# Moving a mode switch four tiles later, and splitting the last three tiles' heads differently, in a bias + logsumexp kernel

## Chip, cores, metric

One NeuronCore of a Trainium2 chip. The metric is device time in microseconds (us) of one execution. Ratios are the mean time of one kernel's fast runs over the mean of the other's fast runs of the same rounds, so they are not quite the ratio of the medians quoted beside them.

## The reference

```python
# x: (8, 2048, 2048) fp32 = batch, row, 8 heads of 256;  bias: (8, 256)
x_heads = x.reshape(B, S, H, Dh).transpose(0, 2, 1, 3) + bias[None, :, None, :]
x_tiled = np.repeat(x_heads, 2, axis=2)          # each row's result is written twice
mx = x_tiled.max(axis=-1, keepdims=True)
out = mx.squeeze(-1) + np.log(np.exp(x_tiled - mx).sum(axis=-1))
```

The kernel leaves the maximum out (the inputs are normal draws) and computes log(sum(exp(x + bias))), over 64 tiles of 128 x 2 rows of 2048 numbers, 2.1 MB each.

## The kernel before: the parts concerned

There are three ways to bring the bias in. *Heads below `pe`*: TensorE adds it in its accumulator memory (PSUM), ScalarE exponentiates and sums, one activation per head and row. *Heads from `g0`*: GpSimd adds it in place, ScalarE exponentiates, VectorE reduces. *Heads between*: ScalarE exponentiates x alone and VectorE multiplies by exp(bias): in bulk (`late=True`) by one multiplication and one reduce a tile later, otherwise at once by one weighted sum per head and row (`weigh`), whose result a short second instruction reads out. With `g0=8` no head goes to GpSimd.

```python
BULK = dict(pe=2, g0=4, late=True)
MIXED = dict(pe=1, g0=5, late=False)
PROMPT = dict(pe=2, g0=8, late=False)
#         from tile, mode, halves: each of the two rows loaded and worked on by itself
STAGES = [(0, BULK, False), (49, MIXED, False), (57, MIXED, True), (61, PROMPT, True)]
LAST_CUTS = [[0, 512, 1280, 2048], [0, 512, 1536, 2048]]   # pieces of tile 63's two rows
...
    def later(m, xt, k0, k1, sums):                    # one piece later
        h0 = m["pe"] if m["late"] else m["g0"]
        v = xt[:, k0:k1, h0 * Dh : D]
        exp_inplace(v)
        if m["late"]:
            ...   # VectorE: heads h0 to g0 times exp(bias), in place
        nc.vector.tensor_reduce(out=sums[:, k0:k1, h0:H], ...)
...
    for t in range(T):
        ...
        for k0, k1, c0, c1 in pieces(t):
            if c0 == 0:
                got = add_bias(m, xt, k0, k1)          # TensorE
                if m["g0"] < H:
                    g_add(m, xt, k0, k1)               # GpSimd
            if for_pool:
                for_pool()                             # `later` of the piece before
            ...
                exp_inplace(xt[:, k0:k1, h0 * Dh : h1 * Dh])
            if for_pe and (c0 == 0 or c1 == D):
                for_pe()                               # ScalarE's own heads, a row late
            ...
                        weigh(...)                     # VectorE, per head and row
            # (cut) for_pool and for_pe are set; load(t + 9) follows the release of the buffer
```

The softmax here doesn't subtract the row's maximum and nothing guards it: scores larger than these inputs give would overflow.

## Time and profile before

| | before |
|---|---|
| time, median of 3 runs | 332.10 us (332.07 to 332.19) |
| profiled span | 330.5 us |
| DMA queue | full until about 319 us, loads of x landed by 323 us |
| VectorE's last read-out | 326.01 us |
| store issued; end of the span | 327.13; 330.5 us |

The groups by form give the price of VectorE's work. Columns: line, engine, operation, names, partitions x elements, count, then busy us and mean ns of one, then idle time before it.

```profile
L228 DVE TENSOR_REDUCE R<-xt 128x12 f32<-128x3072 f32 x49 | 164.4, 3355 | 5.8 <-DVE xt L222 1.0
L222 DVE TENSOR_TENSOR xt<-xt,w_ps 128x1024 f32<-128x1024 f32 x49 | 59.6, 1217 | 29.9 <-ACT xt L212 29.8
L240 DVE CUSTOM_DVE_ANT_0 junk<-xt,w_ps 128x256 f32<-128x256 f32 x114 | 40.6, 417 | 1.2 <-ACT xt L212 1.1
```

A bulk tile is one of each of the first two lines, 4.57 us. A weighted sum (third line) lasts 417 ns, but in a run the next starts 343 ns after it; sums of work here use the distance between starts. The order of VectorE's work and the end of the kernel are shown in the prediction.

### The profile page before, as it was taken

How to read it: one execution, taken by the hardware profiler on the slowest of the kernel's cores; microseconds unless marked ns; L12 is line 12 of the kernel's file. 1: busy time of each engine (PE TensorE's matmuls, PEld its weight loads, DVE VectorE, ACT ScalarE, POOL GpSimd, SP SyncE). 2: the span in 40 equal slices, each digit the busy share in tenths (PEclk: the TensorE clock that was granted, in tenths of full speed). 3: DMA queues.
4: the chain of work that ended last, by engine and by line, in shares of the span. 5: the costliest groups of instructions: out<-in, count | busy, mean ns of one | idle time of the engine just before them, and what ended most of it. 6: DMA issues, size and time to landing. Idle time of an engine off the chain costs nothing.

```text
span 330.5 us, 2287 instructions
## 1 busy us (share of the span) xinstructions
PE 228.9 (69%) x383; PEld 65.3 (20%) x383; DVE 288.3 (87%) x380; ACT 291.4 (88%) x567; POOL 270.7 (82%) x79
## 2 busy tenths in 40 slices
PE   6498675695759667689667796866686645665780
PEld 2132121121212221222211221221121110132220
DVE  0019999999999999999999999998889999999994
ACT  3279999899999999989999889998999998999894
POOL 6999999979989999899999999988998667786300
PEclk9997977579775977955898558777857555555585
DMA  7999999999999999999999999999999999999970
GB/s 293 433 426 434 426 429 426 430 424 428 420 435 425 430 428 426 431 427 430 425 428 426 428 428 428 428 428 427 428 428 429 426 432 415 421 420 421 418 277 17
DMA packets 11744, 135.42 MB, mean 410 GB/s; under 512 B 1425, under 2 KB 1553, under 8 KB 2769
## 3 DMA queue, kind: packets, MB, share of 16 engines
q1 hardware_dynamic: 11632, 135.27, 96.9%
q14 instruction: 11, 0.09, 0.1%
q8 instruction: 3, 0.05, 0.1%
q10 hardware_dynamic: 2, 0.01, 0.0%
q0 software_dynamic: 96, 0.00, 0.0%
HBM read 134.23 MB, written 1.05 MB: 409 GB/s over the span
## 4 chain that ended last, share of the span: by engine, by line
DMA 61%; ACT 14%; issue 7%; POOL 6%; PE 6%; DVE 5%; DVEq 0%; POOLq 0%; SPq 0%; ACTq 0%
DMA xt<-in_x_dram 58%; ACT xt L212 10%; PE ps L177 4%; POOL xt L207 4%; ACT ps L189 4%; DVE xt L222 3%; DVE R L228 2%; DMA b<-bparts 2%; PE ps L167 1%; DMA brow<-in_bias_dram 1%; DVE junk L240 1%; POOL brest L132 0%; POOL brest L130 0%; POOL b L135 0%; PE tpair L258 0%
## 5 line engine op out<-in xcount | busy, mean ns | idle before, releaser
L207 POOL TENSOR_TENSOR xt<-xt,b_rep 128x2048 f32<-128x2048 f32 (+2 forms) x65 | 264.3, 4068 | 35.9 <-DMA xt<-in_x_dram 26.9
L177 PE MATMUL ps<-xt,ident 128*128 128x512 f32 (+1 forms) x240 | 174.6, 859 | 72.1 <-DMA xt<-in_x_dram 71.7
L212 ACT ACTIVATE xt<-xt 128x3072 f32<-128x3072 f32 (+3 forms) x89 | 184.6, 2095 | 10.0 <-POOL xt L207 8.1
L228 DVE TENSOR_REDUCE R<-xt 128x12 f32<-128x3072 f32 (+1 forms) x56 | 176.6, 3154 | 5.8 <-DVE xt L222 1.0
L189 ACT ACTIVATE ps<-ps 128x256 f32<-128x256 f32 x232 | 85.7, 369 | 15.5 <-PE ps L177 10.8
L222 DVE TENSOR_TENSOR xt<-xt,w_ps 128x1024 f32<-128x1024 f32 x49 | 59.6, 1217 | 29.9 <-ACT xt L212 29.8
L177 PEld LDWEIGHTS ps<-xt,ident 128*128 128x128 f32 x240 | 53.5, 252 | 153.9 <-DMA xt<-in_x_dram 113.6
L167 PE MATMUL ps<-b,ones 3*128 3x512 bf16 (+1 forms) x120 | 48.7, 471 | 9.9 <-ACT ps L189 6.0
L189 ACT ACTIVATION_READ_ACCUMULATOR ps<-ps 128x1 f32 x232 | 44.1, 190 | 0.0
L240 DVE CUSTOM_DVE_ANT_0 junk<-xt,w_ps 128x256 f32<-128x256 f32 x114 | 40.6, 417 | 1.2 <-ACT xt L212 1.1
L167 PEld LDWEIGHTS <-ones 3*128 3x128 bf16 x120 | 7.8, 98 | 79.7 <-issue 79.7
L228 DVE TENSOR_REDUCE R_last<-xt 128x3 f32<-128x768 f32 (+1 forms) x9 | 9.4, 1042 | 0.0
L258 PE MATMUL tpair<-ident,R 128*64 128x128 f32 x14 | 3.7, 360 | 7.7 <-DVE R L228 6.2
L240 DVE CUSTOM_DVE_ANT_0 junk<-xt,w_sb 128x256 f32<-128x256 f32 x18 | 6.7, 422 | 0.0
L240 DVE DVE_READ_ACCUMULATOR2_ANT R_last<- 128x1 f32 x76 | 6.5, 85 | 0.0
L139 PE MATMUL ps<-brow,ones 1*128 1x512 f32 x4 | 3.7, 1088 | 3.2 <-DMA brow<-in_bias_dram 3.2
L145 ACT ACTIVATE b_rep<-ps 128x512 f32<-128x512 f32 x2 | 1.2, 598 | 4.4 <-PE ps L139 4.4
L240 DVE DVE_READ_ACCUMULATOR2_ANT R<- 128x1 f32 x56 | 4.7, 84 | 0.0
L268 ACT ACTIVATE res<-tpair 64x512 f32<-64x512 f32 x7 | 4.1, 581 | 0.4 <-PE tpair L258 0.4
L139 PE MATMUL w_ps<-brow,ones 1*128 1x512 f32 x4 | 4.0, 1096 | 0.7 <-ACT w_ps L151 0.7
L258 PEld LDWEIGHTS tpair<-ident,R 128*64 128x64 f32 x14 | 1.4, 134 | 14.9 <-DVE R L228 11.9
L151 ACT ACTIVATE w_ps<-w_ps 128x512 f32<-128x512 f32 x2 | 1.2, 582 | 3.3 <-PE w_ps L139 3.3
(21 smaller groups left out, 12.4 us busy)
## 6 DMA issues: line engine op xcount, KB each, us to landing
xt<-in_x_dram SPq DMA_DIRECT2D x57, 2048.0 KB, 31.8
xt<-in_x_dram SPq DMA_DIRECT2D x12, 1024.0 KB, 20.8
out_dram<-res SPq DMA_DIRECT2D x7, 128.0 KB, 31.3
xt<-in_x_dram SPq DMA_DIRECT2D x3, 256.0 KB, 15.7
xt<-in_x_dram SPq DMA_DIRECT2D x2, 384.0 KB, 15.9
xt<-in_x_dram SPq DMA_DIRECT2D x1, 512.0 KB, 12.2
out_dram<-res_last SPq DMA_DIRECT2D x1, 128.0 KB, 1.7
b<-bparts POOLq DMA_DIRECT2D x3, 1.0 KB, 5.8
```

The source lines that it names most:

```text
L139: nc.tensor.matmul(dst, lhsT=ones, rhs=brow[:, c0:c1], start=True, stop=True)
L145: nc.scalar.activation(out=b_rep[:, c - G0 : c - G0 + MM], in_=ps[i], func=ACT.Copy)
L167: nc.tensor.matmul(p[:, 0 : (kb - ka) * n], lhsT=ones3, rhs=each_row(b3, 0, n, kb - ka), start=True, stop=False,)
L177: nc.tensor.matmul(bass.AP(tensor=p.tensor, offset=p.offset, ap=[p.ap[0], [1, (kb - ka) * n]]), lhsT=ident, rhs=xt[:, ka:kb, 0:n], start=F ...
L189: nc.scalar.activation(out=p[:, c : c + Dh], in_=p[:, c : c + Dh], func=ACT.Exp, accum_out=dst(h),)
L207: nc.gpsimd.tensor_tensor(out=v, in0=v, in1=each_row(b_rep, c - G0, D - c, k1 - k0), op=ALU.add)
L212: nc.scalar.activation(out=v, in_=v, func=ACT.Exp)
L222: nc.vector.tensor_tensor(out=f, in0=f, in1=each_row(w_ps, h0 * Dh - W0, n, k1 - k0), op=ALU.mult,)
L228: nc.vector.tensor_reduce(out=sums[:, k0:k1, h0:H], in_=v.rearrange("p k (h j) -> p k h j", j=Dh), op=ALU.add, axis=mybir.AxisListType.X,)
L240: nc.vector.tensor_tensor_reduce(out=j, in0=v, in1=w, scale=1.0, scalar=0.0, op0=ALU.mult, op1=ALU.add, accum_out=dst,)
L258: nc.tensor.transpose(out=tp[0:nr, k], in_=R[b][:, k].rearrange("p h n -> p (h n)"), identity=ident,)
L268: nc.scalar.activation(out=rs[0:nr], in_=tv, func=ACT.Ln)
```

## The change

Its intent, as I read it: the tail showed VectorE waiting for ScalarE, so ScalarE is given one head less in every other row of the last three tiles; the last row's first piece shrinks to what TensorE needs of it, and the other cuts of the last tile move with the heads; and bulk mode, with fewer VectorE instructions, is kept four tiles longer.

```diff
-PROMPT = dict(pe=2, g0=8, late=False)
-STAGES = [(0, BULK, False), (49, MIXED, False), (57, MIXED, True), (61, PROMPT, True)]
-LAST_CUTS = [[0, 512, 1280, 2048], [0, 512, 1536, 2048]]
+PROMPT2 = dict(pe=2, g0=8, late=False)
+PROMPT1 = dict(pe=1, g0=8, late=False)
+STAGES = [
+    (0, False, (BULK,)),
+    (53, False, (MIXED,)),
+    (57, True, (MIXED, MIXED)),
+    (61, True, (PROMPT2, PROMPT1)),      # row 0, row 1
+]
+LAST_CUTS = [[0, 512, 1024, 2048], [0, 256, 1280, 2048]]
```

The rest of the diff (cut) only makes the mode depend on the row as well.

## The prediction

> **What bounds the kernel now.** I first looked at the page's busy shares and slices. The load queue is full for 38 of the 40 slices, VectorE for nearly as many.
>
> ```profile
> PE 228.9 (69%) x383; PEld 65.3 (20%) x383; DVE 288.3 (87%) x380; ACT 291.4 (88%) x567; POOL 270.7 (82%) x79
> DVE  0019999999999999999999999998889999999994
> DMA  7999999999999999999999999999999999999970
> ```
>
> The reader is to see that the transfer of x (134.23 MB) fills the DMA engines until about 320 us of a span of 330.5 us. Nothing in the change alters the bytes, so until there the time is the transfer's. What can move is the stretch from the last landings to the end. Second, I listed all instructions from 311 us on, to see what ends last:
>
> ```profile
> 322.87 1.57 ACT L212 ACTIVATE xt<-xt 128x1024 f32<-128x1024 f32 x2
> 326.01 0.08 DVE L240 DVE_READ_ACCUMULATOR2_ANT R_last<- 128x1 f32 x1
> 326.24 0.45 PE L276 MATMUL tpair<-ident,R_last 128*128 128x128 f32 x1 [4.25 <-DVE R_last L240]
> 326.72 0.38 ACT L282 ACTIVATE res_last<-tpair 128x256 f32<-128x256 f32 x1 [1.40 <-PE tpair L276]
> 327.13 0.35 SPq L283 DMA_DIRECT2D out_dram<-res_last  x1
> ```
>
> The last row's exponentials on ScalarE, then VectorE's weighted sums up to 326.01, then a transpose, a logarithm and the store: 4.5 us from VectorE's last read-out to the end of the span. VectorE's end sets the kernel's end. Third, VectorE's waits, in 250 to 312 us (first line) and in 300 to 331 us (second):
>
> ```profile
> DVE xt L222 <- ACT xt L212: 0.2, 1, 0.2
> DVE junk L240 <- ACT xt L212: 1.1, 3, 0.4
> ```
>
> From 254.55 us on VectorE waits for nothing until the last rows: it works off a backlog for 64 us, and the 1.1 us of waiting comes only at the very end. So I read its order of work through that stretch; first instruction of a tile or row in each line:
>
> ```profile
> 249.72 1.21 DVE L222 TENSOR_TENSOR xt<-xt,w_ps 128x1024 f32<-128x1024 f32 x1
> 254.55 1.22 DVE L222 TENSOR_TENSOR xt<-xt,w_ps 128x1024 f32<-128x1024 f32 x1 [0.16 <-ACT xt L212]
> 255.87 3.35 DVE L228 TENSOR_REDUCE R<-xt 128x12 f32<-128x3072 f32 x1
> 259.14 0.41 DVE L240 CUSTOM_DVE_ANT_0 junk<-xt,w_ps 128x256 f32<-128x256 f32 x1
> ...
> 276.71 0.41 DVE L240 CUSTOM_DVE_ANT_0 junk<-xt,w_ps 128x256 f32<-128x256 f32 x1
> ...
> 294.27 0.41 DVE L240 CUSTOM_DVE_ANT_0 junk<-xt,w_ps 128x256 f32<-128x256 f32 x1
> ...
> 312.07 0.42 DVE L240 CUSTOM_DVE_ANT_0 junk<-xt,w_ps 128x256 f32<-128x256 f32 x1
> ```
>
> Tile 48, the last bulk one, starts at 254.55; tile 49, the first mixed one, at 259.14; tile 53 at 276.71; the half-tile rows of tile 57 at 294.27; the prompt rows of tile 61 at 312.07. Bulk tiles come at the transfer's pace: multiplications at 239.87, 244.77, 249.72 and 254.55 are 14.68 / 3 = 4.89 us apart, with 4.57 us of work in each and a short wait for ScalarE. Mixed tiles, backlogged, take (294.27 - 259.14) / 8 = 4.39 us. So in mixed mode VectorE gains 0.5 us a tile on the transfer, which in bulk mode it does not. The backlog exists because a bulk tile's sum is done one tile late and a mixed tile's first heads at once: at the switch both fall due together. Tile 49's exponential ended near 256.2, VectorE got to it at 259.14, 2.9 us behind; by tile 61 it was 0.6 us behind.
>
> **What the Trainium skill says.** "VectorE: DVE Perf Modes", section "Mode 1× (REGULAR) — the baseline", makes fp32 or PSUM operands a case of one result per cycle, at 0.96 GHz by its Specifications. 1024, 3072 and 256 elements are then 1.07, 3.20 and 0.27 us; the trace has 1.22, 3.35 and 0.42 us (0.343 us from start to start in a run), so it agrees with some 0.15 us fixed for each, and no faster form is waiting in this change. "ScalarE: Activation LUTs", "What ACT_TABLE_LOAD costs", gives 186 ns + 0.833 ns an element, with about 93 ns overlap: 1.47 us for 1536 elements, the trace 1.479 us. I use it for the one size before has not: 1792 elements, 1.68 us (estimate), 1.59 us from start to start. "GPSIMD Engine Reference", "1. Specifications", says that its SBUF interface is shared with VectorE, with contention for instructions with two SBUF inputs. Only heads 5 to 7 weighted on VectorE read both inputs from SBUF, and GpSimd's last addition ended at 309.3 us, so the trace has no case, and none should arise.
>
> **The change, part by part.**
>
> *Bulk mode to tile 53.* Four tiles swap eight weighted sums and a reduce of 1536 (4.39 us on VectorE when backlogged) for a multiplication and a reduce of 3072 at the transfer's pace of 4.89 us. GpSimd adds 2048 instead of 1536 columns, 4.54 instead of 3.45 us, still under 4.89. ScalarE does two more heads per tile's rows from PSUM; bulk tiles keep pace already. On the path is only VectorE: it reaches tile 53 at 259.14 + 4 x 4.89 = 278.70, not 276.71: +1.99 us. From there on it has fewer mixed tiles in which to catch up, and I expect it never to wait again.
>
> *Alternating two and one ScalarE heads in tiles 61 to 63.* In each odd row one head goes from ScalarE (activation and read-out, some 0.5 us) to VectorE (0.343 us) and into the big exponential (256 x 0.833 ns = 0.21 us). ScalarE is relieved of 0.3 us in each of three rows; VectorE gets 3 x 0.343 = +1.03 us. TensorE has less to do.
>
> *Cuts.* Row 0 of the last tile: exponentials of 512 and 1024 instead of 768 and 768. Row 1: first piece 256, then 1024 and 768 instead of 1024 and 512. The bytes are equal. The narrow piece needs no exponential, only TensorE. If ScalarE were the bound, its last rows would run: row 1 of tile 62 from 317.34 to 318.93, sums of two rows to 320.3, last tile's 512 and 1024 to 321.8, its sums to 322.7, then 1024 and 768 to 324.5. Before, the last exponential ended at 324.43, too. So ScalarE ends as it did.
>
> *The sum for VectorE*, from 278.70: four mixed tiles 4 x 4.39 = 17.57; eight half-tile rows of tiles 57 to 60 at (312.07 - 294.27) / 8 = 2.225, 17.80; then six and seven heads in turn for three tiles, 39 x 0.343 = 13.39 (tile 61's first six took 2.06 us). 278.70 + 17.57 + 17.80 + 13.39 = 327.46, where the last read-out begins; before 326.01. Is it ever idle? It reaches tile 61 at 314.07 (its exponential is done near 311.5), row 1 at 316.13 (ready 314.0), tile 62 at 318.53 (ready 316.4) and 320.59 (318.9), the last tile at 322.99 (320.9), its last row at 325.05 (1024 columns ready at 323.7) and that row's last three heads at 326.4 (ready 324.5). Never. Told as differences: +1.99 for the late start, +1.03 for three more heads, and -1.58 for the idle time that before had after 312.07 (13.94 us for 36 heads of 0.343 = 12.36) and that the backlog now fills: +1.44 us. The close of transpose, logarithm and store is unchanged. 332.1 + 1.44 = 333.5 us.
>
> **Rivals.**
>
> *ScalarE is the bound and is relieved.* This must be the intent: at the end VectorE did wait 1.1 us for it. If the backlog did not reach the last tile, ScalarE would reach the last row's pieces at 322.7 instead of 322.87, but seven heads instead of six follow: VectorE's end +0.15 us, and the time 332.2. With luck in how the last pieces land, 331.7. Against it: the unbroken VectorE of 64 us, which gets two microseconds more to carry.
>
> *Buffers come free later and the load queue starves.* Releases for the last loads move by up to 2 us (tile 52's buffer at 278.8 instead of 276.7). A starving queue would add up to 2 us and give 335 to 336. Against it: landings are 4.89 us apart, a full load lands 31.8 us after issue in the table of issues, so over six tiles are outstanding; and in before the half loads are held by earlier loads' landings, not by buffers. I count nothing.
>
> *The last narrow pieces land later.* Rows of 1 KB may move less well than 2 KB. Before, the last pieces landed near 322.5. A delay by 0.5 us would hide behind VectorE, which is a microsecond and more behind the data. Worth 0 to 0.3 us.
>
> *VectorE's bulk start drifts.* If the transfer's phase or a hiccup puts tile 53 at 278.2 or 279.2, the end moves one for one, as there is no idle time left to take it up: 333.0 to 334.0.
>
> **Range and chances.** The sum rests on durations that repeat to 0.01 us and on one choice, that backlog holds to the end. I leave 0.5 us each way for the start and up to 0.3 for landing, and some room for ScalarE's rival below: 332.4 to 334.4. Two per cent is 6.6 us, and no rival reaches it. Same is 0.975.
>
> **What would show it.** Right: VectorE without a wait from about 274 us to its end; tile 53's first weighted sum at 278.7; tile 61's at 314.1, two microseconds later than before; 39 weighted sums from there to the end; VectorE's waits for ScalarE in the tail gone, and the chain that ended last made of VectorE and no longer of ScalarE; ScalarE's last exponential still near 324.5; DMA landings as before. Wrong: waits of VectorE for ScalarE after 314 us (then the first rival), or a queue with gaps in the last eight slices (the second), or tile 53 at 277 or earlier, which would mean that bulk tiles can be worked faster than the transfer brings them.

## The result, and the profile after

333.46 us (333.30 to 333.56, 4 runs) against 332.13 us (4 runs) in the same rounds: ratio 1.0040, 95% interval 1.0022 to 1.0057. It is slower by 1.3 us, far within 2%.

The page of the changed kernel, its shares and two slice rows:

```profile
PE 231.2 (70%) x395; PEld 68.0 (21%) x395; DVE 289.3 (87%) x326; ACT 291.5 (88%) x573; POOL 275.0 (83%) x79
DVE  0019999999999999999999899998899899999995
DMA  8999999999999999999999999999999999999950
```

The busy shares are nearly unchanged and tell nothing: VectorE's busy time differs by 1.0 us in total. The load queue has no gap. Next VectorE's waits, in 262 to 332 us (columns: who waited for whom, us in total, times, longest), and its order, first instruction of tile 52, of tile 53, of tile 57, of tile 61, and the last:

```profile
DVE xt L228 <- ACT xt L218: 0.9, 3, 0.4
```

```profile
274.27 1.22 DVE L228 TENSOR_TENSOR xt<-xt,w_ps 128x1024 f32<-128x1024 f32 x1 [0.22 <-ACT xt L218]
...
278.87 0.41 DVE L246 CUSTOM_DVE_ANT_0 junk<-xt,w_ps 128x256 f32<-128x256 f32 x1
...
296.44 0.41 DVE L246 CUSTOM_DVE_ANT_0 junk<-xt,w_ps 128x256 f32<-128x256 f32 x1
...
314.24 0.41 DVE L246 CUSTOM_DVE_ANT_0 junk<-xt,w_ps 128x256 f32<-128x256 f32 x1
...
327.64 0.08 DVE L246 DVE_READ_ACCUMULATOR2_ANT R_last<- 128x1 f32 x1
```

All three waits are bulk multiplications, the last at 274.27. From there VectorE works for 53 us without a wait, to the end; before's three waits in the tail are gone. Tile 53 begins at 278.87 instead of 276.71. The close:

```profile
322.45 1.78 ACT L218 ACTIVATE xt<-xt 128x1024 f32<-128x1024 f32 x2
...
327.86 0.45 PE L282 MATMUL tpair<-ident,R_last 128*128 128x128 f32 x1 [5.39 <-DVE R_last L246]
328.34 0.38 ACT L288 ACTIVATE res_last<-tpair 128x256 f32<-128x256 f32 x1 [3.72 <-PE tpair L282]
328.75 0.35 SPq L289 DMA_DIRECT2D out_dram<-res_last  x1
```

ScalarE is done with the last row's exponentials at 324.23 (322.45 + 1.78) and, after its last sum, waits 3.72 us for the end, 1.40 us in before. VectorE is 1.63 us later than before's, the span only 1.15 us longer: the step from the store's issue to the end was 2.88 us, in before 3.35 us. The prediction had taken that as unchanged.

### The profile page after: what moved, and what is told of

It is laid out like the page before. It is cut to its first block, busy times and chain, and to the rows that moved or that the text cites. A ratio compares the mean times of both kernels' runs of the same rounds, so it can differ in the third digit from the quotient of the medians.

```text
span 331.6 us, 2275 instructions
## 1 busy us (share of the span) xinstructions
PE 231.2 (70%) x395; PEld 68.0 (21%) x395; DVE 289.3 (87%) x326; ACT 291.5 (88%) x573; POOL 275.0 (83%) x79
## 5 line engine op out<-in xcount | busy, mean ns | idle before, releaser
L213 POOL TENSOR_TENSOR xt<-xt,b_rep 128x2048 f32<-128x2048 f32 (+2 forms) x65 | 268.6, 4134 | 31.2 <-DMA xt<-in_x_dram 29.1
L183 PE MATMUL ps<-xt,ident 128*128 128x512 f32 (+1 forms) x248 | 177.3, 849 | 69.0 <-DMA xt<-in_x_dram 68.4
L218 ACT ACTIVATE xt<-xt 128x3072 f32<-128x3072 f32 (+4 forms) x85 | 183.2, 2172 | 11.2 <-POOL xt L213 9.2
L234 DVE TENSOR_REDUCE R<-xt 128x12 f32<-128x3072 f32 (+1 forms) x56 | 183.0, 3268 | 6.2 <-DVE xt L228 1.0
L195 ACT ACTIVATE ps<-ps 128x256 f32<-128x256 f32 x237 | 87.5, 369 | 13.5 <-PE ps L183 9.2
L228 DVE TENSOR_TENSOR xt<-xt,w_ps 128x1024 f32<-128x1024 f32 x53 | 64.4, 1216 | 31.3 <-ACT xt L218 31.3
L183 PEld LDWEIGHTS ps<-xt,ident 128*128 128x128 f32 x248 | 56.0, 255 | 151.9 <-DMA xt<-in_x_dram 104.0
L195 ACT ACTIVATION_READ_ACCUMULATOR ps<-ps 128x1 f32 x237 | 45.0, 190 | 0.0
L246 DVE CUSTOM_DVE_ANT_0 junk<-xt,w_ps 128x256 f32<-128x256 f32 x85 | 30.2, 412 | 0.0
```

What stands on the lines that cost most here:

```text
L183: nc.tensor.matmul(bass.AP(tensor=p.tensor, offset=p.offset, ap=[p.ap[0], [1, (kb - ka) * n]]), lhsT=ident, rhs=xt[:, ka:kb, 0:n], start=F ...
L195: nc.scalar.activation(out=p[:, c : c + Dh], in_=p[:, c : c + Dh], func=ACT.Exp, accum_out=dst(h),)
L213: nc.gpsimd.tensor_tensor(out=v, in0=v, in1=each_row(b_rep, c - G0, D - c, k1 - k0), op=ALU.add)
L218: nc.scalar.activation(out=v, in_=v, func=ACT.Exp)
L228: nc.vector.tensor_tensor(out=f, in0=f, in1=each_row(w_ps, h0 * Dh - W0, n, k1 - k0), op=ALU.mult,)
L234: nc.vector.tensor_reduce(out=sums[:, k0:k1, h0:H], in_=v.rearrange("p k (h j) -> p k h j", j=Dh), op=ALU.add, axis=mybir.AxisListType.X,)
```

## The experiments

The theory: VectorE runs a backlog from the switch out of bulk mode to the end, so its end is its start at the switch plus the sum of its work, less what idle time is left. (A backlog is work whose inputs are ready before the engine comes to it.) The main rival: ScalarE's last exponentials set the end. All twelve kernels gave correct results. Here "last read-out" is the start of VectorE's last instruction and "store to end" the time from the store's issue to the last instruction of the trace, both from each profile, in us. (The expectations, and the figures 2.8 and 3.4 us in them, took the second from spans rounded to 0.1 us.) The time before in the same rounds was 332.23 to 332.26 us.

| run | time, us | ratio (95%) | last read-out | store to end |
|---|---|---|---|---|
| before | 332.13 | | 326.01 | 3.35 |
| changed | 333.46 | 1.0040 (1.0022-1.0057) | 327.64 | 2.88 |
| bulk to 53 alone | 332.42 | 1.0005 (0.9993-1.0018) | 326.64 | 2.88 |
| tail alone | 332.26 | 1.0000 (0.9987-1.0012) | 325.83 | 3.33 |
| changed, old cuts | 333.59 | 1.0039 (1.0026-1.0051) | 327.80 | 2.88 |
| changed, bulk to 51 | 332.88 | 1.0021 (1.0007-1.0034) | 326.73 | 3.25 |
| changed, ScalarE loaded | 333.56 | 1.0040 (1.0027-1.0052) | 327.76 | 2.88 |
| before, ScalarE loaded | 333.78 | 1.0045 (1.0031-1.0059) | 327.54 | 3.34 |
| changed, bulk to 45 | 332.51 | 1.0008 (0.9996-1.0021) | 326.65 | 2.88 |
| two heads in tile 63 | 332.02 | 0.9990 (0.9977-1.0002) | 325.84 | 3.33 |
| changed, VectorE filled | 333.60 | 1.0042 (1.0028-1.0056) | 327.98 | 2.88 |
| before, VectorE filled | 332.87 | 1.0019 (1.0006-1.0031) | 326.50 | 3.35 |
| before, TensorE filled | 332.26 | 0.9998 (0.9982-1.0014) | 326.08 | 3.35 |
| changed, TensorE filled | 333.45 | 1.0037 (1.0022-1.0052) | 327.50 | 2.88 |

### Each half of the change alone

```diff
# bulk to 53 alone, on the kernel before
-STAGES = [(0, BULK, False), (49, MIXED, False), ...
+STAGES = [(0, BULK, False), (53, MIXED, False), ...
```

> Bulk mode to tile 53 alone, with before's prompt rows and cuts. Backlog theory (VectorE's unbroken work sets the end): VectorE reaches tile 53 at 278.8 us instead of 276.7 (+2.0), but 1.6 us of its idle time in the tail takes that up: 278.8 + 17.57 + 17.80 + 36 x 0.343 = 326.5, +0.45 us on before, so 332.6 us, and no wait of VectorE after 275 us. Rival (ScalarE's last exponentials set the end): 332.1 us. Rival (late start costs in full, one for one): 334.1 us.

```diff
# tail alone, on the changed kernel
-    (53, False, (MIXED,)),
+    (49, False, (MIXED,)),
```

> Alternating heads and new cuts, bulk mode only to tile 49 as in before. Backlog theory: VectorE reaches tile 61 at 312.1 as before, its three extra heads (1.03 us) fill idle time, and it then waits for ScalarE's 1024 columns of the last row near 323.5; seven heads from there give 326.0, so 332.1 us, within 0.3 of before. Rival (three extra heads add in full): 333.1 us. Rival (ScalarE's relief pays): 331.7 us or less.

Bulk to 53 alone: 332.42 us. The last lines of its VectorE and its queue:

```profile
326.64 0.08 DVE L240 DVE_READ_ACCUMULATOR2_ANT R_last<- 128x1 f32 x1
327.76 0.35 SPq L283 DMA_DIRECT2D out_dram<-res_last  x1
```

VectorE ends 0.63 us later than in before, near the 0.45 expected, and does not wait after 280 us. Of its 2.2 us later start (278.90) the idle time took up 1.6. Of the 0.63 us only 0.2 shows in the time, as this run, too, has the shorter close. That a late start costs in full is excluded: 0.63 us is not 2.2 us.

Tail alone: 332.26 us, as before. Its only wait in the tail, and its last read-out:

```profile
318.84 0.42 DVE L246 CUSTOM_DVE_ANT_0 junk<-xt,w_ps 128x256 f32<-128x256 f32 x1 [0.37 <-ACT xt L218]
...
325.83 0.08 DVE L246 DVE_READ_ACCUMULATOR2_ANT R_last<- 128x1 f32 x1
```

Three more heads on VectorE were free here, as expected. But the place of the wait was not the expected one: not the last row's 1024 columns near 323.5, but the second row of tile 62, at 318.84. From there 20 heads follow without a gap, 318.84 + 20 x 0.343 = 325.7. So neither half costs anything clear of noise, 0.2 and 0.0 us, and together they cost 1.3. Before has 1.6 us of idle time in the tail. The three heads alone live on it; the late start alone uses it up, and the 0.63 us that it leaves over are nearly hidden by the shorter close. With the idle time spent, the three heads cost their full price: 327.64 - 326.64 = 1.00 us, against 3 x 0.343 = 1.03.

### The cuts

```diff
# the changed kernel
-LAST_CUTS = [[0, 512, 1024, 2048], [0, 256, 1280, 2048]]
+LAST_CUTS = [[0, 512, 1280, 2048], [0, 512, 1536, 2048]]
```

> The changed kernel with before's cuts of the last rows. Backlog theory: cuts are hidden behind VectorE's backlog, 333.4 us, within 0.15 of the changed kernel; last weighted sum again near 327.3. Rival (narrow pieces cost in the transfer, or help ScalarE): 0.3 us or more away from the changed kernel, in either direction.

333.59 us, ratio 1.0039 where the changed kernel had 1.0040; VectorE's end 327.80, with tile 53 begun 0.16 us later (279.03). The cuts do nothing while VectorE is behind.

### How far the switch lies

```diff
# the changed kernel
-    (53, False, (MIXED,)),
+    (51, False, (MIXED,)),      # and in another run 45
```

> The changed kernel with bulk mode to tile 51, half way. Backlog theory: VectorE reaches tile 51 at 268.9 us; 6 x 4.39 + 17.80 + 39 x 0.343 follow, 326.5 us, so 332.6 us: one microsecond less backlog than the changed kernel, without a wait at the end or with less than 0.3 us of it. Rival (the switch's position does not matter, the tail does): 333.4 us.

> The changed kernel with bulk mode to tile 45 only. Backlog theory: eight mixed tiles more than the changed kernel leave no backlog at tile 61, VectorE waits for ScalarE in several of the last rows, and its end is ScalarE's, as with tile 49: 332.2 us, no gain from 49 to 45. Rival (half a microsecond less for each tile, without a floor): 330.2 us.

At 51: last read-out 326.73, 0.2 us over the expectation, as tile 51 began at 269.17, not 268.9; time 332.88, 0.3 us over it. With the same tail, VectorE's end for a switch at 49, 51 and 53 is 325.83, 326.73 and 327.64: 0.45 us per tile of bulk mode, against 4.89 - 4.39 = 0.50 by the pace of the two modes. (The run with 49 has a wait, so only the step from 51 to 53, 0.91 us for two tiles, lies between two runs that never wait in the tail.) At 45 it gains nothing more: 332.51 us. VectorE's weighted sums now wait for ScalarE in three places of the tail,

```profile
312.05 0.42 DVE L246 CUSTOM_DVE_ANT_0 junk<-xt,w_ps 128x256 f32<-128x256 f32 x1 [0.42 <-ACT xt L218]
314.62 0.42 DVE L246 CUSTOM_DVE_ANT_0 junk<-xt,w_ps 128x256 f32<-128x256 f32 x1 [0.42 <-ACT xt L218]
319.65 0.42 DVE L246 CUSTOM_DVE_ANT_0 junk<-xt,w_ps 128x256 f32<-128x256 f32 x1 [0.48 <-ACT xt L218]
```

the last again at tile 62's second row, and 319.65 + 20 x 0.343 = 326.5. So there is a floor, and it lies where the data sets it: in this profile that row's data let TensorE begin at 317.94, against 317.13 in the tail-only run, which puts VectorE's end 0.8 us later than there; the shorter close takes back 0.45 us, and the time came out 0.3 us over the expectation. The moment at which the same data land differs by up to 0.8 us between these two profiles, for a cause that I did not look for.

### Is ScalarE on the path?

```diff
             if for_pool:
                 for_pool()
                 for_pool = None
+            if t == T - 2:
+                nc.scalar.activation(out=spare, in_=b_rep, func=ACT.Exp)   # result unused
# (cut) spare is allocated above
```

> The changed kernel with two needless exponentials of 1024 columns on ScalarE in tile 62's rows (1.9 us of its time, some 0.5 us of it in an idle gap). If ScalarE is off the path, as the backlog theory has it, VectorE is still later than ScalarE by 0.3 us or more everywhere and the time stays at 333.5 us (within 0.3). Rival (ScalarE shares the bound): 334.5 us or more.

> The same two needless exponentials in the kernel before, where I hold ScalarE's last rows to set when VectorE ends: +1.7 us, 333.8 us, and VectorE's waits for ScalarE in the tail grow. If VectorE's own work set the end in before too, it would stay at 332.2 us.

This tells the theory from the main rival most directly. In the changed kernel: 333.56 us, ratio 1.0040, the same as without. ScalarE's last row moved by 1.27 us, from 322.45 to 323.72, and VectorE still did not wait once after 280 us:

```profile
323.72 1.78 ACT L219 ACTIVATE xt<-xt 128x1024 f32<-128x1024 f32 x2
...
327.76 0.08 DVE L247 DVE_READ_ACCUMULATOR2_ANT R_last<- 128x1 f32 x1
```

In before the same two instructions cost 1.5 us, and VectorE's waits in the tail (280 to 332 us) grew from 1.1 us to

```profile
DVE junk L241 <- ACT xt L213: 2.7, 4, 1.1
```

So in before ScalarE sets the end and in the changed kernel VectorE does. The change moved the bound from the one to the other and overshot.

### A candidate

```diff
# the changed kernel
-    (53, False, (MIXED,)),
+    (49, False, (MIXED,)),
     (57, True, (MIXED, MIXED)),
     (61, True, (PROMPT2, PROMPT1)),
+    (63, True, (PROMPT2, PROMPT2)),
# and before's LAST_CUTS
```

> A candidate: bulk mode to tile 49, tiles 61 and 62 alternate between two and one heads, tile 63 has two in both rows and before's cuts. ScalarE comes to the last row 0.4 us earlier than in before and VectorE has six heads there, not seven: VectorE ends near 325.5 us instead of 326.0, 331.7 us. If only total work of VectorE counts, it is between before and the tail-only run: 332.2 us.

332.02 us, ratio 0.9990 with an interval that holds 1. VectorE ended at 325.84, not 325.5: its data and so tile 62's second row came later (VectorE's wait ended at 319.19), and 19 heads from there give 325.7. It may be a little faster than before; these runs do not show it.

### The shorter close

By then every run with bulk mode to tile 53 or 45 had 2.88 us from the store's issue to the end, every run to tile 49 or 51 3.25 to 3.35 us; so it does not simply go with the length of bulk mode. I tried the length of two engines' programs.

```diff
     nc.vector.memset(ones3, 1.0)
+    for _ in range(54):
+        nc.vector.memset(spare, 0.0)          # 1 x 16; (cut) allocated above
```

> The changed kernel with 54 idle writes of 16 numbers on VectorE at the start, where it has nothing to do for 16 us, so that its program is as long as before's. From the store's issue to the end of the span it took 3.4 us in the runs with bulk mode to tile 49 and 2.9 us in those to tile 53, and these differ by 54 to 66 instructions of VectorE. If the length of VectorE's program decides it: 3.3 us to 3.4 us here, and 333.9 us. If it is anything else: 2.9 us and 333.5 us.

> The kernel before with the same 54 idle writes: as many VectorE instructions as the run with bulk mode to tile 45 (436 against 448), which had 2.8 us from the store to the end. If the length of VectorE's program decides: 2.8 us to 2.9 us and 331.7 us. If it is anything else: 3.4 us and 332.2 us.

```diff
+    for _ in range(12):
+        nc.tensor.matmul(tps[0][:, 0], lhsT=ones3, rhs=ones3, start=True, stop=True)
     n_ps = [0]
```

> The kernel before with 12 needless small matmuls (3x128 by 3x128, bf16) at the start, where TensorE waits for the bias's three parts. TensorE then has as many instructions as the changed kernel, 395 matmuls. So far every run with 395 had 2.8 us to 2.9 us from the store's issue to the end of the span, every run with 383 had 3.3 us to 3.4 us. If the length of TensorE's program decides it: 2.9 us here, 331.8 us. If it is anything else: 3.4 us and 332.2 us.

> The changed kernel with the same 12 small matmuls, 407 in all. If the length of TensorE's program decides the store's time to the end and comes and goes with it (371: 2.8 us, 383: 3.4 us, 395: 2.9 us), 3.3 us to 3.4 us and 333.9 us. If it is anything else: 2.9 us and 333.5 us.

Both ideas fell. The filled kernels kept the close of the kernels that they were made from: 2.88 us (changed) and 3.35 us (before), with VectorE filled and with TensorE filled.

The traces, read instruction by instruction (`prof` leaves the closing ones out), show where the difference lies: in SyncE, the engine that issues the loads of x and the stores and that waits for the last store. In before it stands still from 2.10 to 2.47 us after the store's issue, between two closing instructions. All seven runs with a long close have such a pause of 0.34 to 0.37 us there, none of the seven with 2.88 us has one. It always follows SyncE's 207th recorded instruction. SyncE has 211 recorded instructions in before (and 215 with bulk mode to 51, where the pause comes earlier in the close, at 1.83 us), the last 11 of them after the store, so the 207th is part of the close. In the changed kernel it has 219, and the 207th comes 11 us before the store, where SyncE waits anyway; with bulk mode to 45 it has 206 and never gets there. So it goes with the length of the third engine's program, SyncE's. All fourteen traces agree; no run lengthened SyncE's program alone, and what SyncE does in the pause is not shown.

That VectorE-filled before took 332.87 us was expected by neither idea. VectorE waits for ScalarE there (1.6 us in the tail, before 1.1), and the data were later: TensorE began tile 62's second row at 317.87, not 317.36, and VectorE's end was 326.50. In the changed kernel with VectorE filled they were late as well (317.91, not 317.24). Why is open.

## Why the prediction was right, by its steps

- **Bulk tiles keep the transfer's pace, so VectorE reaches tile 53 late.** Predicted 278.70, measured 278.87. The late start was +2.16 us where +1.99 was predicted; why it was 0.17 us more was not looked for. (The prediction's first line counts 38 full slices of the load queue; the row of digits has 37. Nothing rests on it.)
- **No idle time from there.** Right: no wait after 274.27. From the start of tile 53 to the last read-out: 327.64 - 278.87 = 48.77 us, predicted 17.57 + 17.80 + 13.39 = 48.76.
- **Differences.** Predicted +1.99 + 1.03 - 1.58 = +1.44; measured +2.16 for the start and 13.40 - 13.94 = -0.54 from tile 61 on (predicted +1.03 - 1.58 = -0.55), together +1.62 of the 1.63 by which VectorE's end moved. That the terms are of this kind is shown by the two halves run alone: 0.63 us with only the first and third, and no loss where the heads went into idle time.
- **The close unchanged.** Wrong by half a microsecond: 2.88 us from store to end instead of 3.35, as SyncE's pause no longer falls there. Together with the later start this left +1.15 us in the profiled spans and +1.33 us in the times, against +1.44. That the predicted 333.5 us is so near the measured 333.46 us is in part luck: two misses of opposite sign.
- **Cuts hidden, ScalarE's end as before.** Right: 324.23 against 324.43 us, and the old cuts give the same time.
- **Releases later, no starving.** Right: the DMA row of the slices has no gap.
- **The rivals.** ScalarE as the bound of the changed kernel is refuted by loading it. The rival's figure for the case without a backlog, 332.2 us, was nearly met (332.26 us, tail alone), but by another wait than the one named: the prediction took the last row's pieces as the limit; it is tile 62's second row, after which VectorE's 20 heads leave no gap.
- **The skill.** "ScalarE: Activation LUTs", section "What ACT_TABLE_LOAD costs", led to 1.68 us (estimate) for 1792 columns; the trace has 1.70 us. "GPSIMD Engine Reference", "1. Specifications", on sharing with VectorE: no run here shows it, as GpSimd was idle by then.

## What to carry to other kernels

Where an engine works off a backlog, look for the place where the backlog starts, not for the place where its end is felt: its end is that start plus the sum of its work. Idle time in a tail is a budget that parts of a change share, so test the parts alone and together. Before giving work to the engine that waits at the end, find out whether it waits for lack of work or only because it caught up just in time.

## What the Trainium skill lacked or had wrong

- The close (it would belong to "Runtime: NRT & Kernel Launch"): no page that I read says that it can hold a pause of 0.34 to 0.37 us, according to the length of SyncE's program. From the last store's issue to the end of the span took 2.88 us without the pause and 3.25 to 3.35 us with it; the length of VectorE's or TensorE's program made no difference in the four runs that changed it.
- No page that I read says that a full load queue can deliver the same data at different moments in different profiles: tile 62's second row let TensorE begin at 317.1 to 317.9 us in the profiles that I compared.
